# S5 input matrices built in their final layout from factors read back from DRAM, and adaLN pieces summed in PSUM

## The chip, the cores and the metric

One Trainium2 chip, one core. The metric is the device time of one call in microseconds (us). Engines are named as in the profile: PE (TensorE matmul), PEld (its weight load), DVE (VectorE), ACT (ScalarE), POOL (GpSimd), SP (SyncE, which here only issues DMAs).

## What is computed

Two layers of a diffusion backbone over 384 token columns (128 context, 256 latent), width 1024. Layer 0 is half-SwiGLU, S5 mixer, half-SwiGLU; layer 1 has an RG-LRU in the middle. Each sub-layer's shift, scale and gate come from a linear map of the conditioning vector ("adaLN"). What the change touches is the S5 mixer's preparation and that map:

```
abar     = exp(dt * a);  q = (abar - 1) / a           # complex, per direction, group, state
bb       = q[..., None] * b                           # 64 groups x 64 states x 16 inputs
s[t]     = abar * s[t-1] + bb @ u[t]                  # forward and backward
y        = c_re @ s_re - c_im @ s_im + d * u
mod      = silu(cond) @ ada_w + ada_b                 # shift, scale, gate
```

The kernel runs the recurrence in blocks of 8 tokens. For that it needs, for each of the 64 groups, a matrix E (8 x 16 inputs to 64 states of two directions, real and imaginary: powers of abar times bb), a matrix G (states to outputs) and the taps inside a block.

## The kernel before

Matmuls are exact to float32 by splitting each operand into a high and a low part and summing three products (`mm3`, L264 to L266). Weights stream through `raw` buffers (SP queue), ACT makes the high part (L253), DVE the low part (L256). PE's instructions are placed by hand, in program order; the order on DVE, POOL and SP is made by a scheduler from priorities, and each engine executes its queue in that order.

The stage in question is the first feed-forward block, `ffn(0, ...)`. While its matmuls run, a generator `s5_tables` prepares the S5 matrices. Between matmuls `ffn` calls `side()` (made by `beside`): every second k of an up-projection, every third of a down-projection. There are 124 calls before `gen_done()`, which runs the rest of the generator at once, and one more fill comes after it. A call does either one `ada_fill()` (four small matmuls of one adaLN chunk of weights) or one step of the generator, at reduced priority. `beside(125, 42, 9)` means 42 fills spread over 125 calls; the first nine are taken at the even calls 2 to 18.

The generator's steps: three of them (`PRO`) make the elementwise tables (L567 to L684: exp, sine, cosine, powers, `pe`, `pg`, and q in `sn` and `cs`). They are given out before the first matmuls, with no PE work in them. Then come, for 16 chunks of four groups:

- `build_e`: loads `s5bc`, makes bb = q b (six DVE operations of 64 elements per partition, L645 to L650 in `cmul`) and E (six of 512), with states on the partitions;
- `store_e`: eight PE transposes (L731) in two groups of four, two ACT copies (L732), a store to DRAM (`etd`, L734, POOL's queue);
- `taps`: 32 small matmuls (L742) of bb and G, which leave `ks`;
- `build_g`: three DVE and three POOL operations of 640 elements (L716 to L722) and a store (`gd`).

E's buffer (`ech`) exists once, so the next E is written when the transposes have read the last. Nine steps without work stand between the first `build_e` and the first `store_e`; each chunk takes five steps.

`ada_fill` sums the two k-halves of a piece in PSUM, and adds the pieces of a group (four, or two in the first sub-layer) in SBUF: the first by an ACT copy (L151), the others by a DVE addition (L153). Six chunks remain for the S5 stage and are filled there in the middle of its outputs (`ADAS = 4, 2`).

Of the kernel before, what the change touches and what calls it, by code (L numbers as in the profile page):

```python
# [23 lines left out]
Q = 8  # L24
# [10 lines left out]
ADAS = 4, 2  # L35
# [10 lines left out]
def backbone(ctx, tc, a, o):  # L46
# [60 lines left out]
    ada_acc = [None, None, 0]  # L107
# [22 lines left out]
    def ada_fill(n=1, load=True, bank=psaux, flush=True):  # L130


        for _ in range(n):
# [14 lines left out]
            if kh == 1:  # L148
                if j == 0:
# [4 lines left out]
                if j == len(group) - 1:  # L154
                    ada_pend.append((l, s, group, ada_acc[1]))
# [400 lines left out]
    kd = dram.tile([2048, 240], F32, name="kd")  # L556
    td = dram.tile([128, 64, 128], F32, name="td")
# [26 lines left out]
    def s5_tables(gp_):  # L584
# [91 lines left out]
        pe = gp_.tile([128, 2, 8, 64], F32, name="s5pe")  # L676
# [10 lines left out]
        def build_e(ch):  # L687
            g0 = ch * 4
            bc = gp_.tile([128, 4, 64], F32, name="s5bc", tag="bc", bufs=2)
            nc.sync.dma_start(bc, a["s5bc"][ch])  # L690
            ncr = gp_.tile([128, 64], F32, name="s5ncr", tag="ncr")
            V.tensor_scalar(ncr, bc[:, 2, :], -1.0, None, op0=OP.mult)
            bb = gp_.tile([128, 2, 80], F32, name="s5bb", tag="bb", bufs=2)
            G.memset(bb[:, :, 64:80], 0.0)

            qv = lambda t: vw(t, g0, [[1, 4], [0, 16]])
            bv = lambda ri: vw(bc, ri * 64, [[16, 4], [1, 16]])
            ov = lambda ri: vw(bb, ri * 80, [[16, 4], [1, 16]])
            cmul(ov(0), ov(1), qv(sn), qv(cs), bv(0), bv(1), [[16, 4], [1, 16]])

            E = gp_.tile([128, 4, 2, 128], F32, name="s5E", tag="ech")
            pv = lambda ri: vw(pe, ri * 512 + g0, [[1, 4], [64, 8], [0, 16]])
            bv = lambda ri: vw(bb, ri * 80, [[16, 4], [0, 8], [1, 16]])
            ov = lambda ri: vw(E, ri * 128, [[256, 4], [16, 8], [1, 16]])
            cmul(ov(0), ov(1), pv(0), pv(1), bv(0), bv(1), [[128, 4], [16, 8], [1, 16]])
            return bc, ncr, bb, E

        def build_g(ch, bc, ncr):
# [4 lines left out]
            cv = lambda t, j: vw(t, j * 64, [[16, 4], [0, 10], [1, 16]])  # L713
            ov = lambda ri: vw(Gt, ri * 160, [[320, 4], [16, 10], [1, 16]])
            p = [vw(tp, j * 640, [[160, 4], [16, 10], [1, 16]]) for j in range(2)]
            V.tensor_tensor(p[0], cv(bc, 2), pv(0), op=OP.mult)  # L716
            V.tensor_tensor(p[1], cv(bc, 3), pv(1), op=OP.mult)
            V.tensor_tensor(ov(0), p[0], p[1], op=OP.subtract)
            p = vw(tq, 0, [[160, 4], [16, 10], [1, 16]])
            G.tensor_tensor(ov(1), cv(ncr, 0), pv(1), op=OP.mult)  # L720
            G.tensor_tensor(p, cv(bc, 3), pv(0), op=OP.mult)
            G.tensor_tensor(ov(1), ov(1), p, op=OP.subtract)  # L722
            nc.gpsimd.dma_start(gd[ch].rearrange("p (b c) -> p b c", c=128), vw(Gt, 16, [[160, 8], [1, 128]]))
            return Gt

        def store_e(ch, E):
            eo = gp_.tile([128, 1024], F32, name="s5eo", tag="eo")
            for j in range(2):
                pt = psum()
                for b in range(4):  # L730
                    PE.transpose(pt[:, b * 128:b * 128 + 128], E[:, j * 2 + b // 2, b % 2, :], ident)  # L731
                S.activation(eo[:, j * 512:j * 512 + 512], pt, AF.Copy)  # L732
                yield
            nc.gpsimd.dma_start(etd[ch], eo)  # L734

        def taps(ch, bb, Gt):

            kx = (psum(), psum())
            for ri in range(2):
                for d in range(2):  # L740
                    for q in range(4):
                        PE.matmul(kx[d][32 * q:32 * q + 32, 0:128], bb[64 * d:64 * d + 64, ri, q * 16:q * 16 + 32],  # L742
# [8 lines left out]

        cur = build_e(0)
        Gt = build_g(0, *cur[:2])
# [41 lines left out]
    def s5(i, prev):  # L795
        l, s3 = divmod(i, 3)
        with ExitStack() as st:
# [41 lines left out]
            with ExitStack() as st2:  # L839
# [89 lines left out]
                with tc.manual_schedule(engines={ET.Pool}):  # L929
# [5 lines left out]
                    with tc.manual_schedule(engines={ET.DVE, ET.Activation, ET.SP}):  # L935
# [28 lines left out]
                        ada_load(6, nc.sync)  # L964
# [13 lines left out]
                        for part, m in ((f, 0), (f, 1), (f, 2), (s_, 0), (s_, 1), (y, 0), (s_, 2), (f, 3), (f, 4), (y, 1),  # L978
# [3 lines left out]
                            if part is y:  # L982
# [10 lines left out]
                                if m in (2, 3):  # L993
                                    ada_fill(ADAS[m - 2], False, psum, False)
# [350 lines left out]
def _layout(inp):  # L1345
# [34 lines left out]
    gb = lambda v: np.concatenate([v.transpose(1, 0, 2).reshape(64, 16, 4, 16)] * 2, 0)  # L1380
    ct = lambda v: gb(v.transpose(0, 2, 1))
    A["s5bc"] = np.stack([gb(f("s5_b_re")[0]), gb(f("s5_b_im")[0]), ct(f("s5_c_re")[0]), ct(f("s5_c_im")[0])],
# [43 lines left out]
```

## Time and profile before

| | |
|---|---|
| median of 3 runs | 1631.84 us (1628.37 to 1637.66) |
| profiled execution | 1631.38 us, span 1629.6 us |
| PE busy | 1546.1 us (95%) |
| DVE busy | 1278.5 us (78%) |
| ACT busy | 709.4 us (44%) |
| POOL busy | 336.5 us (21%) |
| mean granted PE clock | 0.974 |

A matmul's own duration (0.34 us) overlaps the next; what one costs is the distance from one start to the next. A DVE operation's duration overlaps the next one by some 0.08 us. The granted clock is 1.00 at 2.4 GHz and 0.5 at 1.2 GHz; a figure between is a mean over a stretch.

### The profile page before, as it was taken

To read this page: it belongs to the slowest core of one execution; us is meant where nothing else is said; L and a number is where in the kernel's file an instruction comes from. 1 tells how busy PE (TensorE), PEld (TensorE's weight loads), DVE (VectorE), ACT (ScalarE), POOL (GpSimd) and SP (SyncE) were. 2 spreads that over 40 slices of the span, in tenths; PEclk is the share of its full clock that TensorE was granted. 3 is DMA by queue.
4 is the path that set the end of the run, shared out by engine and by line. 5 is a ranking of instruction groups with operands and counts; after the bars stand their busy time and mean duration, and the time that the engine had idled before them with its cause. 6 is when DMAs were issued, how large, how long until landed. Compare 5 with 4: busy or idle time off the path is not lost.

```text
span 1629.6 us, 25853 instructions
## 1 busy us (share of the span) xinstructions
PE 1546.1 (95%) x9554; PEld 1474.6 (90%) x9554; DVE 1278.5 (78%) x2750; ACT 709.4 (44%) x1157; POOL 336.5 (21%) x524
## 2 busy tenths in 40 slices
PE   7989999999988999999999999999989599999996
PEld 5877887889988999999999999999978599999995
DVE  4999999977796569979777998977797889644445
ACT  4423332335655366333345632334569366323332
POOL 0155445423380013000002300000165322000001
PEclk9989999999999999999999999999999799999997
DMA  9766776877878533667556356755513243544321
GB/s 352 260 215 224 232 244 237 259 244 275 129 272 257 201 133 118 230 202 243 173 171 208 117 188 214 243 193 160 193 64 118 76 157 123 160 153 139 100 77 39
DMA packets 108543, 301.19 MB, mean 185 GB/s; under 512 B 28384, under 2 KB 40160, under 8 KB 108160
## 3 DMA queue, kind: packets, MB, share of 16 engines
q1 hardware_dynamic: 85792, 249.62, 46.3%
q0 software_dynamic: 13152, 46.70, 8.7%
q10 hardware_dynamic: 9472, 3.21, 1.4%
q8 instruction: 75, 1.23, 0.3%
q14 instruction: 52, 0.43, 0.1%
HBM read 275.89 MB, written 27.80 MB: 186 GB/s over the span
## 4 chain that ended last, share of the span: by engine, by line
PE 70%; DVE 20%; DMA 3%; issue 3%; ACT 3%; POOL 1%; SPq 0%; ACTq 0%; DVEq 0%; POOLq 0%
PE mm L264 22%; PE mm L266 22%; PE mm L265 22%; DVE lo L256 2%; DVE hl L317 1%; PE aux L144 1%; DMA adaw<-in_ada_w 1%; DVE s5sb L881 1%; DVE w L878 1%; DVE w L460 1%; ACT w L322 1%; DVE lxc L1090 1%; PE mm L917 1%; DVE s5sb L880 1%; DVE w L879 1%
## 5 line engine op out<-in xcount | busy, mean ns | idle before, releaser
L264 PE MATMUL mm<-hh,hi 128*128 128x384 f32 (+1 forms) x1568 | 542.1, 346 | 14.5 <-DVE hh L1143 7.3
L265 PE MATMUL mm<-hl,hi 128*128 128x384 f32 (+1 forms) x1568 | 535.7, 342 | 10.2 <-DVE hl L317 10.1
L266 PE MATMUL mm<-hh,lo 128*128 128x384 f32 (+1 forms) x1568 | 535.4, 341 | 5.0 <-DVE lo L256 5.0
L253 ACT ACTIVATE hi<-raw 128x1024 fp32r<-128x1024 f32 (+1 forms) x332 | 323.2, 976 | 495.7 <-PE mm L265 467.1
L256 DVE TENSOR_TENSOR lo<-raw,hi 128x1024 fp32r<-128x1024 f32 (+1 forms) x344 | 393.6, 1148 | 164.4 <-ACT hi L253 154.1
L264 PEld LDWEIGHTS mm<-hh,hi 128*128 128x128 f32 x1568 | 298.7, 191 | 32.9 <-issue 15.7
L265 PEld LDWEIGHTS mm<-hl,hi 128*128 128x128 f32 x1568 | 299.0, 191 | 13.3 <-DVE hl L317 12.7
L266 PEld LDWEIGHTS mm<-hh,lo 128*128 128x128 f32 x1568 | 298.6, 190 | 7.0 <-DVE lo L256 7.0
L264 PE MATMUL mm<-zh,hi 128*128 128x384 f32 x704 | 240.5, 342 | 2.0 <-ACT zh L479 2.0
L265 PE MATMUL mm<-zl,hi 128*128 128x384 f32 x704 | 237.5, 337 | 1.8 <-DVE zl L480 1.6
L266 PE MATMUL mm<-zh,lo 128*128 128x384 f32 x704 | 237.0, 337 | 0.0
L264 PEld LDWEIGHTS mm<-zh,hi 128*128 128x128 f32 x704 | 132.9, 189 | 9.6 <-issue 6.3
L179 DVE SCALAR_TENSOR_TENSOR dump<-raw,cb 128x512 bf16<-128x512 f32 x160 | 109.9, 687 | 39.7 <-DMA raw<-in_ada_t 39.2
L265 PEld LDWEIGHTS mm<-zl,hi 128*128 128x128 f32 x704 | 133.1, 189 | 2.6 <-DVE zl L480 2.6
L266 PEld LDWEIGHTS mm<-zh,lo 128*128 128x128 f32 x704 | 133.2, 189 | 0.0
L479 ACT ACTIVATE zh<-w 128x384 fp32r<-128x384 f32 x88 | 46.1, 525 | 160.5 <-DVE w L487 154.1
L179 DVE SCALAR_TENSOR_TENSOR raw<-raw,cb 128x512 f32<-128x512 f32 x160 | 110.1, 688 | 2.6
L395 POOL TENSOR_TENSOR t<-mv 128x3 f32<-128x3 f32 x5 | 4.0, 799 | 446.0 <-ACT mv L394 446.0
L264 PE MATMUL mm<-ph,hi 128*128 128x388 f32 x224 | 77.4, 346 | 0.0
L265 PE MATMUL mm<-pl,hi 128*128 128x388 f32 x224 | 76.6, 342 | 0.0
L266 PE MATMUL mm<-ph,lo 128*128 128x388 f32 x224 | 76.3, 341 | 0.0
L545 DVE SCALAR_TENSOR_TENSOR r<-mm,gate,r 128x128 f32<-128x128 f32 (+1 forms) x144 | 53.2, 410 | 20.5 <-PE mm L266 20.5
(356 smaller groups left out, 1983.1 us busy)
## 6 DMA issues: line engine op xcount, KB each, us to landing
raw<-in_up SPq DMA_DIRECT2D x176, 512.0 KB, 4.4
raw<-in_ada_t SPq DMA_DIRECT2D x80, 512.0 KB, 4.2
raw<-in_down SPq DMA_DIRECT2D x56, 512.0 KB, 3.9
adaw<-in_ada_w POOLq DMA_DIRECT2D x42, 512.0 KB, 5.3
adaw<-in_ada_w SPq DMA_DIRECT2D x22, 512.0 KB, 7.9
raw<-in_down SPq DMA_DIRECT2D x48, 192.0 KB, 2.4
gd<-s5G POOLq DMA_DIRECT2D x16, 512.0 KB, 4.8
etd<-s5eo POOLq DMA_DIRECT2D x16, 512.0 KB, 5.5
```

Of the source, the lines that this page charges most:

```text
L144: PE.matmul(acc[32 * q:32 * q + 32, :256], cond[:, kh * 4 + q, 6 - 2 * j:38 - 2 * j], w[:, q, :], start=kh == 0, stop=kh == 1, tile_positi ...
L179: V.scalar_tensor_tensor(out, wq, 1.0, cb[:, g, q * 512:q * 512 + 512], op0=OP.mult, op1=OP.mult, accum_out=part[:, t, g, q:q + 1])
L253: S.activation(hi[:, :n], raw[:, :n], AF.Copy)
L256: V.tensor_tensor(lo[:, :n], raw[:, :n], hi[:, :n], op=OP.subtract)
L264: PE.matmul(ps, hi[:, c:c + 128], xh, start=start, stop=False)
L265: PE.matmul(ps, hi[:, c:c + 128], xl, start=False, stop=False)
L266: PE.matmul(ps, lo[:, c:c + 128], xh, start=False, stop=stop)
L317: V.tensor_tensor(hl[:, k, :n], src, hh[:, k, :n], op=OP.subtract)
L322: S.activation(h[:, c0:c1], r[:, k, c0:c1], AF.Identity, bias=bs[:, k, g:g + 1], scale=gs[:, k, g:g + 1])
L460: V.scalar_tensor_tensor(t[:, c0:c1], self.ms[:, c0:c1], gw[:, g:g + 1], t[:, c0:c1], op0=OP.mult, op1=OP.add)
L479: S.activation(zh, z, AF.Copy)
L545: V.scalar_tensor_tensor(r[:, m, c0:c1], ps[:, c0:c1], gate[:, m, g:g + 1], r[:, m, c0:c1], op0=OP.mult, op1=OP.add)
```

## The change

- E is made with rows (token in block, input) on the partitions, as it is stored. Its two factors are spread over the partitions by DMA: `pt`, the powers times q, and `bt`, the input b. For `pt` the product `pq` = pe q is made once for all groups, transposed once (eight PE transposes, two ACT copies) and stored to a scratch tensor `ptd`; each chunk then reads its 4 KB row of each of the eight tokens into 16 partitions. E is stored straight from its buffer. The transposes and ACT copies of each chunk are gone.
- bb = q b is made for eight groups at a time (six operations of 128 elements, every second chunk). The negated c moves from DVE to POOL.
- A chunk takes four steps instead of five; two new steps (`pq`; its transposes) stand ahead of the chunks, and six empty steps instead of nine.
- `ada_fill` keeps one PSUM bank over all pieces of a group and empties it once. 40 fills go beside `ffn(0)`, eight into the S5 stage (`ADAS = 4, 4`), with one more chunk loaded ahead and one during the outputs.

```
-ADAS = 4, 2
+ADAS = 4, 4
...
-            if kh == 0:
-                if flush:
-                    ada_flush(bank)
-                ada_acc[0] = bank()
+            if kh == 0 and flush:
+                ada_flush(bank)
             acc = ada_acc[0]
+            begin = acc is None
+            if begin:
+                acc = ada_acc[0] = bank()
+            done = kh == 1 and j == len(group) - 1
+            end = done or close and x == n - 1
...
-                          start=kh == 0, stop=kh == 1, tile_position=(0, 32 * q))
+                          start=begin, stop=end, tile_position=(0, 32 * q))
...
+        pq = gp_.tile([128, 2, 8, 64], F32, name="s5pq", tag="pt")
...
+        cmul(pv(pq, 0), pv(pq, 1), pv(pe, 0), pv(pe, 1), qv(sn), qv(cs), [[64, 8], [1, 64]])
+        yield
+        rows = gp_.tile([128, 2, 4, 128], F32, name="s5rows", tag="ech")
+        for ri in range(2):
+            ps = psum()
+            for b in range(4):
+                PE.transpose(ps[:, b * 128:b * 128 + 128], pq[:, ri, 2 * b:2 * b + 2, :].rearrange("p s g -> p (s g)"), ident)
+            S.activation(rows[:, ri].rearrange("p b c -> p (b c)"), ps, AF.Copy)
+            nc.gpsimd.dma_start(ptd.rearrange("(b s) g r p -> r (s g) b p", s=2)[ri], rows[:, ri])
+        yield
+
+        def load_e(ch):
+            pt = gp_.tile([128, 1024], F32, name="s5pt", tag="pt")
+            nc.sync.dma_start(pt, bass.AP(ptd.tensor, ptd.offset + ch * 1024, [[16384, 8], [0, 16], [1, 1024]]))
+            bt = gp_.tile([128, 512], F32, name="s5bt", tag="bt")
+            nc.sync.dma_start(bt, bass.AP(a["s5bt"].tensor, a["s5bt"].offset + ch * 8192, [[0, 8], [512, 16], [1, 512]]))
+            return pt, bt
...
+            cmul(pv(E, 0), pv(E, 1), pv(pt, 0), pv(pt, 1), bv(0), bv(1), [[128, 4], [64, 2], [1, 64]])
+            nc.gpsimd.dma_start(etd[ch], E.rearrange("p g r c -> p (g r c)"))
...
+            G.tensor_scalar(ncr, two["s5c"][:, 0, ch % 2 * 64:ch % 2 * 64 + 64], -1.0, None, op0=OP.mult)
...
-        for _ in range(9):
+        fac = load_e(0)
+        scaled(0)
+        Gt = build_g(0)
+        for _ in range(6):
             yield
         for ch in range(16):
-            yield from store_e(ch, cur[3])
-            nxt = build_e(ch + 1) if ch < 15 else None
+            build_e(ch, *fac)
+            if ch < 15:
+                fac = load_e(ch + 1)
             yield
-            taps(ch, cur[2], Gt)
             yield
-            if nxt:
-                Gt = build_g(ch + 1, *nxt[:2])
-            cur = nxt
+            taps(ch, two["bb"], Gt)
+            if ch % 2 and ch < 15:
+                scaled(ch // 2 + 1)
+            yield
+            if ch < 15:
+                Gt = build_g(ch + 1)
             yield
...
-                        ada_load(6, nc.sync)
+                        ada_load(7, nc.sync)
...
-                                    ada_fill(ADAS[m - 2], False, psum, False)
+                                    ada_fill(ADAS[m - 2], False, psum, False, True)
+                                    if m == 2:
+                                        ada_load(4, nc.sync)
...
-        norm = ffn(0, (8, 7, 7), None, beside(125, 42, 9), gen_done, first)
+        norm = ffn(0, (8, 7, 7), None, beside(125, 40, 9), gen_done, first)
```

`load2` loads `s5b` and `s5c` for eight groups (128 KB each); `scaled` makes bb from `s5b`.

## Rows read from the trace of the kernel before

**Rows 1.** Busy time by stretch: us, engine busy (count), granted clock, DMA share, GB/s.

```profile
core 0: us, PE busy (x) PEld busy (x) DVE busy (x) ACT busy (x) POOL busy (x), PEclk, DMA share, GB/s
82.00:354.00 272.00, 260.88 (x2022) 227.32 (x2022) 261.46 (x423) 86.77 (x143) 125.36 (x143) 0.97 0.72 235
```

**Rows 2.** Instruction groups of 82 to 354 us, PE's waits: busy, mean ns | idle before.

```profile
L264 PE MATMUL mm<-zh,hi 128*128 128x384 f32 x120 | 45.0, 375 | 2.0 <-ACT zh L479 2.0
L265 PE MATMUL mm<-zl,hi 128*128 128x384 f32 x120 | 42.1, 351 | 1.6 <-DVE zl L480 1.5
L731 PE MATMUL mm<-ident,s5E 128*128 128x128 f32 x120 | 20.3, 289 | 5.5 <-DVE s5E L650 4.7 <-DVE s5E L647 0.8
L193 PE MATMUL aux<-c_sel,adae 128*128 128x8 f32 x20 | 2.8, 250 | 2.0 <-DVE adae L153 2.0
```

**Rows 3.** PE in order of time around a fill and a group of transposes.

```profile
201.47 0.34 PE L265 MATMUL mm<-hl,hi 128*128 128x384 f32 x1
201.64 0.34 PE L266 MATMUL mm<-hh,lo 128*128 128x384 f32 x1
...
202.76 0.34 PE L265 MATMUL mm<-hl,hi 128*128 128x384 f32 x1
...
204.50 0.34 PE L266 MATMUL mm<-hh,lo 128*128 128x384 f32 x1
...
205.30 0.34 PE L265 MATMUL mm<-hl,hi 128*128 128x384 f32 x1
```

**Rows 4.** In order of time: the second side call (a fill), and DVE's table operations.

```profile
56.87 0.64 PE L144 MATMUL aux<-adaw,cond 128*32 128x256 f32 x8
...
59.22 0.22 DVE L608 SCALAR_TENSOR_TENSOR s5t<-s5t,s5t 128x64 f32<-128x64 f32 x1
...
77.86 1.47 DVE L680 COPY s5pe<-s5pw 64x512 f32<-64x512 f32 x1
```

**Rows 5.** DVE's instruction groups, each form apart, up to 354 us.

```profile
L649 DVE TENSOR_TENSOR s5tp<-s5pe,s5bb 128x512 f32<-128x512 f32 x16 | 10.9, 683 | 0.0
L645 DVE TENSOR_TENSOR s5tp<-s5pw 128x128 f32<-128x128 f32 x1 | 0.3, 283 | 0.0
L645 DVE TENSOR_TENSOR s5tp<-s5pw 128x64 f32<-128x64 f32 x1 | 0.2, 217 | 0.0
L692 DVE TENSOR_SCALAR s5ncr<-s5bc 128x64 f32<-128x64 f32 x15 | 5.3, 356 | 0.4 <-DMA s5bc<-in_s5bc 0.4
L153 DVE TENSOR_TENSOR adae<-adae,aux 128x256 f32<-128x256 f32 x14 | 5.8, 411 | 1.1 <-PE aux L144 1.1
L256 DVE TENSOR_TENSOR lo<-raw,hi 128x1024 fp32r<-128x1024 f32 x39 | 50.4, 1296 | 0.4 <-ACT hi L253 0.4
L545 DVE SCALAR_TENSOR_TENSOR r<-mm,gate,r 128x128 f32<-128x128 f32 x16 | 5.5, 343 | 0.0
```

**Rows 6.** DVE and POOL side by side, and POOL's group of 640-element operations.

```profile
213.20 1.85 POOL L720 TENSOR_TENSOR s5G<-s5ncr,s5pg 128x640 f32<-128x640 f32 x1
...
213.89 1.25 DVE L645 TENSOR_TENSOR s5tp<-s5t,s5bc 128x64 f32<-128x64 f32 x1
...
215.21 0.21 DVE L646 TENSOR_TENSOR s5tp<-s5t,s5bc 128x64 f32<-128x64 f32 x1
...
L722 POOL TENSOR_TENSOR s5G<-s5G,s5tq 128x640 f32<-128x640 f32 x16 | 28.5, 1780 | 0.7
```

**Rows 7.** PE near the stage's end: the last taps but one, the last fill.

```profile
353.75 0.67 PE L742 MATMUL mm<-s5G,s5bb 64*32 64x128 f32 x32
...
358.12 0.64 PE L144 MATMUL aux<-adaw,cond 128*32 128x256 f32 x8
```

**Rows 8.** PE in the S5 stage: its second place of fills, two chunks.

```profile
508.83 1.07 PE L144 MATMUL mm<-adaw,cond 128*32 128x256 f32 x16
```

**Rows 9.** DMA issues: count, KB each, median us to landing.

```profile
raw<-etd SPq DMA_DIRECT2D x12, 512.0 KB, 6.6
...
s5bc<-in_s5bc SPq DMA_DIRECT2D x16, 128.0 KB, 3.4
```

More of the change, by code (lines that the diff above doesn't have):

```diff
@@ L128, in ada_load, with ada_fill @@
             ada_loaded.append((c, w, extra))
-    def ada_fill(n=1, load=True, bank=psaux, flush=True):
-        for _ in range(n):
+    def ada_fill(n=1, load=True, bank=psaux, flush=True, close=False):
+        for x in range(n):
             if not ada_loaded:
@@ L153, in ada_fill @@
                     V.tensor_tensor(ada_acc[1], ada_acc[1], acc[:, :256], op=OP.add)
-                if j == len(group) - 1:
-                    ada_pend.append((l, s, group, ada_acc[1]))
+                ada_acc[0] = None
+            if done:
+                ada_pend.append((l, s, group, ada_acc[1]))
+                ada_acc[1] = None
     def vec_pool():
@@ L708, in build_g, with load2, scaled @@
-        def build_g(ch, bc, ncr):
+        two = {}
+        def load2(n, b):
+            two[n] = gp_.tile([128, 2, 128], F32, name=n, tag=n)
+            nc.sync.dma_start(two[n], a[n][b])
+        def scaled(b):
+            bt = two["s5b"]
+            bb = gp_.tile([128, 2, 144], F32, name="s5bb", tag="bb", bufs=2)
+            G.memset(bb[:, :, 128:144], 0.0)
+            qv = lambda t: vw(t, b * 8, [[1, 8], [0, 16]])
+            bv = lambda ri: vw(bt, ri * 128, [[16, 8], [1, 16]])
+            ov = lambda ri: vw(bb, ri * 144, [[16, 8], [1, 16]])
+            cmul(ov(0), ov(1), qv(sn), qv(cs), bv(0), bv(1), [[16, 8], [1, 16]])
+            two["bb"] = bb
+            if b < 7:
+                load2("s5b", b + 1)
@@ L710, in build_g @@
+        def build_g(ch):
             g0 = ch * 4
@@ L712, in build_g @@
             pv = lambda ri: vw(pg, ri * 640 + g0, [[1, 4], [64, 10], [0, 16]])
-            cv = lambda t, j: vw(t, j * 64, [[16, 4], [0, 10], [1, 16]])
+            cv = lambda j: vw(two["s5c"], j * 128 + ch % 2 * 64, [[16, 4], [0, 10], [1, 16]])
             ov = lambda ri: vw(Gt, ri * 160, [[320, 4], [16, 10], [1, 16]])
             p = [vw(tp, j * 640, [[160, 4], [16, 10], [1, 16]]) for j in range(2)]
-            V.tensor_tensor(p[0], cv(bc, 2), pv(0), op=OP.mult)
-            V.tensor_tensor(p[1], cv(bc, 3), pv(1), op=OP.mult)
+            V.tensor_tensor(p[0], cv(0), pv(0), op=OP.mult)
+            V.tensor_tensor(p[1], cv(1), pv(1), op=OP.mult)
             V.tensor_tensor(ov(0), p[0], p[1], op=OP.subtract)
             p = vw(tq, 0, [[160, 4], [16, 10], [1, 16]])
-            G.tensor_tensor(ov(1), cv(ncr, 0), pv(1), op=OP.mult)
-            G.tensor_tensor(p, cv(bc, 3), pv(0), op=OP.mult)
+            ncr = z
+            G.tensor_scalar(ncr, two["s5c"][:, 0, ch % 2 * 64:ch % 2 * 64 + 64], -1.0, None, op0=OP.mult)
+            G.tensor_tensor(ov(1), vw(ncr, 0, [[16, 4], [0, 10], [1, 16]]), pv(1), op=OP.mult)
+            G.tensor_tensor(p, cv(1), pv(0), op=OP.mult)
             G.tensor_tensor(ov(1), ov(1), p, op=OP.subtract)
+            if ch % 2 and ch < 15:
+                load2("s5c", ch // 2 + 1)
             nc.gpsimd.dma_start(gd[ch].rearrange("p (b c) -> p b c", c=128), vw(Gt, 16, [[160, 8], [1, 128]]))
             return Gt
[L726 to L734, printed above, removed]
         def taps(ch, bb, Gt):
@@ L741, in taps @@
                     for q in range(4):
-                        PE.matmul(kx[d][32 * q:32 * q + 32, 0:128], bb[64 * d:64 * d + 64, ri, q * 16:q * 16 + 32],
+                        c0 = ch % 2 * 64 + q * 16
+                        PE.matmul(kx[d][32 * q:32 * q + 32, 0:128], bb[64 * d:64 * d + 64, ri, c0:c0 + 32],
                                   Gt[64 * d:64 * d + 64, q, ri, 32 * d:32 * d + 128],
@@ L1379, in _layout @@
     A["s5a"] = np.concatenate([gp(f("s5_a_re")[0]), gp(f("s5_a_im")[0]), gp(ldt)], 1)
[L1380 removed]
+    gb = lambda v: np.concatenate([v.transpose(1, 0, 2).reshape(64, 8, 128)] * 2, 0)
     ct = lambda v: gb(v.transpose(0, 2, 1))
[L1382 to L1383 removed]
+    bt = lambda v: v.transpose(2, 0, 1).reshape(16, 16, 4, 64)
+    A["s5bt"] = np.stack([bt(f("s5_b_re")[0]), bt(f("s5_b_im")[0])], 3).transpose(1, 0, 2, 3, 4).reshape(16, 16, 512)
+    A["s5b"] = np.stack([gb(f("s5_b_re")[0]), gb(f("s5_b_im")[0])], 0).transpose(2, 1, 0, 3)
+    A["s5c"] = np.stack([ct(f("s5_c_re")[0]), ct(f("s5_c_im")[0])], 0).transpose(2, 1, 0, 3)
     dsk = np.zeros((4, 32, 16), np.float32)
```

37 lines of the change are left out of this document (13 added, 24 removed).

## The prediction

> **What bounds the kernel now.** The views were read in this order: the span in slices, busy time by stretch, the groups of the stretch that the change touches, then single places in order of time. The change lies almost wholly in one stretch, from about 55 us (the first side calls) to 358 us (the last fill); behind it only two fills and a few loads move. In the middle of that stretch, 272 us long, PE is busy for 260.9 us and DVE for 261.5 us [rows 1]. Both are full at once, so a saving on one of them alone need not be a gain. Everywhere else PE leads, and nothing there changes.
>
> PE's waits in the stretch are small and nearly all are for DVE: 5.5 us at the transposes for E, 2.0 us at the flush for the piece sums, 2.0 and 1.6 us for the down-projection's operands [rows 2]. The granted clock is 0.97 there [rows 1], so some 3% of 272 us, 8.2 us, went to half-speed time after such waits. Together 19.3 us.
>
> DVE's busy time holds something that is not work. A 64-element operation takes 0.217 us alone [rows 5], but 1.25 us when it meets a POOL operation that has just started; the next one takes 0.21 us [rows 6]. POOL runs three such operations per chunk, 1.78 us each in the group shown [rows 6], and the change leaves all three in place. So fewer DVE instructions do not shorten these blocked times; they fall on whatever DVE runs then.
>
> **The change, part by part. PE.** In a plain stretch matmuls start every 0.175 us (201.47 to 201.64 is 0.17). From the matmul ahead of a group of four transposes to the second one behind it, 204.50 to 205.30, are 0.80 us, of which two plain distances are 0.35: a group costs 0.45 us. A fill costs in the same way 1.12 - 0.35 = 0.77 us [rows 3]. Removed are 32 groups, 14.4 us; added two, 0.9 us; two fills leave for the S5 stage, 1.5 us. PE's work falls by 15.0 us, and the waits for E (5.5 us) lose their place.
>
> **An early wait on PE.** The transposes of `pq` are the generator's fifth step, which is side call 3. Call 2 is the fill at 56.87 us; with it and 12 matmuls, call 3 stands at about 59.5 us. At 59.22 us DVE is still at the cosine's polynomial; it finishes `pe` at 79.3 us [rows 4]. `pq` is six operations of 512 elements, 0.683 us each [rows 5]: 4.1 us, to 83.4 us. When PE stands still, DVE gets no new feed-forward work once the buffers ahead are full, so the earliest end is some 4 us sooner (the four to five operations of the feed-forward block between 59 and 80 us) and the latest some 3 us later (all of them stay, and POOL blocks twice): 79 to 86. I take 82, which is near the row itself: PE waits 22.5 us. Queued behind on PE is all of the feed-forward block. Nothing of before shows this wait, as the tables had no PE instruction behind them until call 19.
>
> **DVE.** From the tables' end to the last G (about 354 us, just ahead of the taps at 353.75 and 357.5 [rows 7]) DVE was busy 261.5 us of 272 [rows 1]. For the same point after the change:
>
> - bb: 96 operations at 0.217 become 48 at 0.283 [rows 5]: -7.2 us.
> - The negated c leaves DVE: 15 at about 0.2 us undisturbed: -3 us (-5.3 with the blocked time in the row [rows 5]). On POOL it comes back as a short operation that may block DVE: 0 to 5.7 us (16 of the row's 0.356), I take +2, as it has a tenth of the elements of the others.
> - The piece sums: -5.8 us [rows 5]; one ACT copy per group remains, and ACT is busy for a third of the time [rows 1].
> - E keeps its six operations of 512 elements, in another order of addresses: 0, since the forms with stride and with broadcast both go down to 0.68 us. But E of chunk 15 isn't needed for the last taps: -4.1 us.
> - The last taps come earlier in the feed-forward block. A chunk takes four generator steps, not five; with 40 fills in 125 calls, taps 15 are generator step 71 and side call 104, while before the last G fell to call 123. DVE must by then have done the block's work of calls 3 to 104 (101 calls), where before it was calls 12 to 123 (111). That work is six groups, from 50.4 to 5.5 us [rows 5], 103 us in all, 0.93 us a call: -9 us.
>
> Sum: 261.5 - 27 = 234.5 us busy. The 10.5 us that DVE was idle may go or stay; I take half: 240 (234 to 245). From 82 us this ends at 322 us. PE needs less: it stood at call 3 at 82 us, and its work to call 104 is about 217 us (54 calls of 12 matmuls, 47 of 7 or 8, 32 fills, 16 taps at 0.8): 299 us. So the taps wait for DVE, and PE stands at call 104 at 322 us. What is queued behind the taps on PE is the feed-forward block; DVE itself starts ahead in it only as far as its buffers.
>
> **The rest of the block.** From call 104 to the fill of call 125 PE has 21 calls of 12 matmuls (44 us), 7 fills (5.4 us) and taps (0.8 us): 50 us. The end is 372 us against 358.1 [rows 7]: +14 us. The S5 stage takes two more chunks at its second place, where two took 1.07 us between outputs [rows 8]: +1.1 us (0 if the two DVE sums that vanish there were what PE waited for, 1.9 at the half clock). Together +15: 1631.4 + 15 = 1646 us. The profiled execution (1631.38) lies 0.5 us under the median, so nothing is corrected.
>
> **Loads.** Each chunk reads 768 KB for `pt` and `bt` in place of 128 KB for `s5bc`. `pt` is loaded when E has read the last one; until the next E DVE has G, taps and feed-forward work, 240 / 16 - 4.1 = 10.9 us. A 512 KB read of a scratch tensor lands after 6.6 us, a 128 KB load after 3.4 [rows 9]. I take 7 to 10 us, so the load is covered, at no cost; it decides from about 10 us.
> The Trainium skill ("DMA: Bandwidth & Descriptors", on why a DMA increments its semaphore by 16, and the rules for kernel authors) speaks against these two loads: a DMA is split over as many engines as divide its slowest dimension, and an outer broadcast of 8 keeps it on at most 8 of 16. No run here shows such a load; by that rule the two would take longer than the rows say, and the third rival below would be the case.
>
> **The rivals.** *PE sets the pace.* If DVE's blocked times shrink with its load, or the scheduler puts E behind the block's own operations, PE runs freely after the early wait. From 59.5 to 358.1 it took 298.6 us; less 15.0 us of work and the 19.3 us of waits and slow clock is 264.3; from 82 us this ends at 346.3, 11.8 us early, with the S5 stage +1.1: 1621 us. For it: PE's own work does fall, and E no longer stands on its way. Against: DVE is full in [rows 1], and would have to get through about 10% less than the sum says.
> *The same, without the early wait*, if the scheduler brings the tables forward: 22.5 us less, 1598 us. Against: DVE was as full before 59 us as behind it.
> *The factors come late.* If `pt` and `bt` land 12 us after the last E, each E and all DVE work behind it starts 2 us later: 15 chunks, 30 us: 1676 us. It decides where landing passes about 10 us; against it stand the medians of [rows 9], for it that the block's loads share the engines.
> That the change doesn't do what it says has no place here: the instructions are gone from the code.
>
> **How the numbers follow.** DVE sets the pace: 0.50, 1646 us, its own range 1633 to 1659 (DVE's sum 234 to 245, the early wait 79 to 86, POOL's extra operation). PE sets the pace: 0.27, 1614 to 1629. Without the early wait: 0.07. Late factors: 0.16, 1655 to 1685. A measurement of this kernel tells about 0.5%, 8 us, from no change. Faster by more than that (under 1623.7): 0.19 of the second case and 0.07, 0.26. Slower (over 1640): 0.40 of the first and 0.16, 0.56. Between: 0.18. The range leaves out about one in ten on either side: 1612 (the third case and the low end of the second) to 1668 (the upper half of the last).
>
> **What would show it.** Right: a PE gap of some 20 us near 60 us, ended by `pq`'s transposes; DVE at 95% or more until the last G; PE waits at the taps or at the low parts between 120 and 320 us; no generator work behind call 104, and some 50 us of undisturbed matmuls after it; E's operations without waits for a DMA. Wrong: no gap at 60 us, or a gap and then no further one; E's first operation waiting for `pt`; blocked DVE operations much rarer than before.

## The result: 80 us slower

The changed kernel takes 1711.49 us (median of 4 runs, 1709.07 to 1713.29) against 1631.82 us (4 runs, 1628.37 to 1637.66): ratio 1.0482, 95% interval 1.0461 to 1.0502. The forecast was 1646 us with a range of 1612 to 1668: the direction was right, the size was not.

The first reading is where the 82 us between the two profiled spans (1629.6 and 1711.5 us) arise. A mark that both kernels have is the sums for the next normalisation, twelve matmuls at the end of the feed-forward block and again at the end of the S5 stage. Before:

```profile
393.37 1.50 PE L388 MATMUL aux<-omean,sum 128*128 128x1 f32 x12
...
600.35 1.50 PE L388 MATMUL aux<-omean,sum 128*128 128x1 f32 x12
```

After (PE in order of time):

```profile
471.25 1.50 PE L394 MATMUL aux<-omean,sum 128*128 128x1 f32 x12
...
682.68 1.50 PE L394 MATMUL aux<-omean,sum 128*128 128x1 f32 x12
```

So 77.9 us are lost in the feed-forward block with the tables, 4.4 us in the S5 stage (207.0 became 211.4 us), and nothing behind it (1029.3 and 1028.8 us to the end). In the stretch of [rows 1] both engines that were full are now idle for a fifth of the time, and the granted clock is 0.88 where it was 0.97 (busy time by stretch, columns as there):

```profile
82.00:354.00 272.00, 216.58 (x1592) 183.80 (x1592) 215.63 (x295) 54.44 (x92) 122.97 (x133) 0.88 0.70 223
```

PE's and DVE's waits between 50 and 460 us say for what (line waited for: us in total, times, longest). PE, against [rows 2]:

```profile
PE mm L726 <- DVE s5pq L654: 23.2, 1, 23.2
PE mm L270 <- ACT zh L485: 17.0, 3, 7.1
PE mm L270 <- DVE w L493: 16.6, 4, 10.2
PE aux L148 <- DMA adaw<-in_ada_w: 11.1, 3, 6.9
```

DVE:

```profile
DVE s5tp L652 <- DMA s5bt<-in_s5bt: 48.6, 12, 8.8
DVE lo L262 <- ACT hi L259: 33.9, 14, 5.2
```

The first line of PE is the forecast early wait. The first line of DVE is the one that the forecast's sum gave no price to: L652 is the first operation of E, and in 12 of 16 chunks it waits for bt (in chunk 0 for pt, 1.9 us). One chunk in order of time (SP's issues, DVE's operations):

```profile
257.74 0.60 SPq L734 DMA_DIRECT2D s5pt<-ptd  x1
258.43 0.61 SPq L736 DMA_DIRECT2D s5bt<-in_s5bt  x1
...
257.74 0.69 DVE L657 TENSOR_TENSOR s5E<-s5tp 128x512 f32<-128x512 f32 x1
...
262.19 0.83 DVE L757 TENSOR_TENSOR s5G<-s5tp 128x640 f32<-128x640 f32 x1
270.49 0.69 DVE L652 TENSOR_TENSOR s5tp<-s5pt,s5bt 128x512 f32<-128x512 f32 x1 [7.48 <-DMA s5bt<-in_s5bt]
```

The loads go out when E has read the last factors, and bt lets DVE go on 12.1 us after its issue (258.43 to 270.49). In between DVE does what stands ahead of E, then stands still for 7.5 us with the feed-forward block's operations queued behind E. pt is not what holds it: by the trace's landing records, pt lands 7.0 us after its issue here and bt, issued 0.7 us behind it, after 11.9. Over all 16 loads of each the medians are 7.8 us for pt (6.4 to 10.3) and 10.5 us for bt (8.2 to 13.1). PE's waits for `zh` and `w` are read as the echo. The loop's pace and the end of the block follow from it (line: count, shortest/median/longest ns, first to last start): the last step of E, the taps, the fills.

```profile
L657 DVE TENSOR_TENSOR s5E<-s5tp x16: 678/692/1820, 103.4 to 385.1; 128x512 f32<-128x512 f32 x16
L776 PE MATMUL mm<-s5G,s5bb x512: 266/269/419, 137.3 to 384.1; 64*32 64x128 f32 x171
L148 PE MATMUL aux<-adaw,cond x448: 379/403/637, 5.0 to 436.7; 128*32 128x256 f32 x150
```

A chunk takes (385.1 - 103.4) / 15 = 18.8 us. The last matmul of the taps starts at 384.1 (357.9 before), that of the fills 52.6 us later, at 436.7 ([rows 7]: 358.1). The forecast was 322 and 372.

### The profile page after: what moved, and what is told of

The parts are those of the page before. It is cut to its first block, busy times and chain, and to the rows that moved or that the text cites. A ratio compares the mean times of both kernels' runs of the same rounds, so it can differ in the third digit from the quotient of the medians.

```text
span 1711.5 us, 25534 instructions
## 1 busy us (share of the span) xinstructions
PE 1549.9 (91%) x9434; PEld 1473.7 (86%) x9434; DVE 1277.8 (75%) x2671; ACT 690.4 (40%) x1127; POOL 346.0 (20%) x532
## 4 chain that ended last, share of the span: by engine, by line
PE 60%; DVE 16%; DMA 5%; issue 3%; ACT 2%; POOL 2%; SPq 0%; ACTq 0%; DVEq 0%; POOLq 0%
PE mm L270 19%; PE mm L272 19%; PE mm L271 19%; DMA s5bt<-in_s5bt 3%; DVE lo L262 2%; DVE hl L323 1%; DMA etd<-s5E 1%; DVE s5sb L919 1%; DVE w L466 1%; DVE w L916 1%; DVE lxc L1130 1%; PE mm L955 1%; DVE r L436 1%; DVE r L437 1%; DVE s5sb L918 1%
## 5 line engine op out<-in xcount | busy, mean ns | idle before, releaser
L262 DVE TENSOR_TENSOR lo<-raw,hi 128x1024 fp32r<-128x1024 f32 (+1 forms) x344 | 402.9, 1176 | 188.3 <-ACT hi L259 177.4
```

Source lines behind the costliest of these rows:

```text
L262: V.tensor_tensor(lo[:, :n], raw[:, :n], hi[:, :n], op=OP.subtract)
```

## The experiments

Times are medians beside runs of the kernel before on the same chip (1632.8 to 1634.0 us). "Mark" is the first of the sums above (393.4 before, 471.3 after). e1, e2, e3, e5, e6 and e7 ran once each. Runs of the kernel before lie between 1628 and 1638 us, so among these six a difference of a few us shows nothing. The theory at the start: late loads cost most of the 65 us beyond the forecast, and they are late because of their shape; the rivals: E's place in DVE's order or DVE's own pace, and the early wait.

**e1, no loads after the first chunk.** `if ch < 15: fac = load_e(ch + 1)` is left out, and with it the right factors for 15 chunks.

> The changed kernel, but the factors (pt and bt) are loaded for chunk 0 alone; E of the other fifteen chunks is computed from the same factors, so fifteen loads of each are left out and those chunks' tables hold other numbers. Late loads (my theory now): in the changed kernel a chunk takes 18.8 us, of which some 11 to 12 are the landing of the loads; without them the cycle falls to DVE's own 15 us (240 us over 16 chunks), 16 x 3.8 = 61 us less, 1645 to 1660 us. Rival, the order of the instructions on DVE (E standing ahead of feed-forward work, whatever it waits for) or POOL's blocking sets the cycle: less than 15 us are gained, over 1695 us.

1668.0 us, mark 426.4. The loads cost 43 us, less than the 50 to 65 expected, and both theories named a part. The lines of E, the taps and the fills:

```profile
L657 DVE TENSOR_TENSOR s5E<-s5tp x16: 677/688/1704, 103.5 to 338.0; 128x512 f32<-128x512 f32 x16
L776 PE MATMUL mm<-s5G,s5bb x512: 269/269/420, 130.9 to 339.3; 64*32 64x128 f32 x171
L148 PE MATMUL aux<-adaw,cond x448: 379/379/637, 5.1 to 391.8; 128*32 128x256 f32 x150
```

A chunk now takes 15.6 us, near the 15 expected for DVE's own pace. But 33 us of the 78 remain in the block, where I had forecast 14, and no load is left to blame.

**e2, the transposes of pq later.** Six generator steps later (the expectation calls them side calls; with the fills between they are more calls), first chunk as before:

```diff
-        yield
+        for _ in range(7):
+            yield
         rows = gp_.tile([128, 2, 4, 128], F32, name="s5rows", tag="ech")
...
-        for _ in range(6):
-            yield
+        yield
         for ch in range(16):
```

> The changed kernel with the transposes of pq six side calls later; the chunks start at the same call as before, so everything is computed. If the early wait of 23 us on PE adds to the rest, the time falls by 15 to 23 us, to 1688 to 1696 us. Rival: the chain of loads and E sets when the block ends, and it starts at the same time as before or later, so that the wait only moves from 60 us to the taps: within 8 us of 1711 us, or slower by the up to 10 us by which the first factors come later.

1708.7 us, mark 465.7: the early wait is gone from PE's list, and 31.3 us of waits for G stand at the taps in its place (1.3 in the changed kernel). The time is 2.8 us less, which a single run does not tell from no change. DVE's chain sets the end, and its end moved by 5 us:

```profile
L657 DVE TENSOR_TENSOR s5E<-s5tp x16: 678/691/2132, 114.9 to 380.3; 128x512 f32<-128x512 f32 x16
```

A wait of 25 us on PE that stands ahead of a stretch paced by DVE was not a cost of its own.

**e3, the same loads with a slowest dimension of 16.** ptd is stored twice (c = 0, 1), bt comes repeated from DRAM:

```diff
-  bass.AP(ptd.tensor, ptd.offset + ch * 1024, [[16384, 8], [0, 16], [1, 1024]])
+  bass.AP(ptd.tensor, ptd.offset + ch * 1024, [[16384, 16], [0, 8], [1, 1024]])
-  bass.AP(a["s5bt"].tensor, ..., [[0, 8], [512, 16], [1, 512]])
+  a["s5bt"][ch]
```

> The changed kernel, everything computed, but the slowest dimension of both factor loads counts 16 and more in place of 8: ptd is stored twice by the two halves of a channel group, so that pt is read as 16 x 8 rows, and bt comes repeated from DRAM as 128 plain rows; bytes written to SBUF are the same. If the loads are late because they run on 8 of the 16 DMA engines, landing falls from 11 to 12 us to 6 to 8 us, the chunk cycle from 18.8 to 15 or 16 us, and the time to 1650 to 1680 us. Rival, they are late because of 768 KB per chunk, of what else is in the queues, or because pt can only be read again once E has read it: landing stays above 10 us and the time within 15 us of 1711 us.

1683.7 us, mark 441.0: 28 us back for the same bytes into SBUF. The DMA list (KB each, median us to landing) and E's line:

```profile
s5pt<-ptd SPq DMA_DIRECT2D x16, 512.0 KB, 6.1
s5bt<-in_s5bt SPq DMA_DIRECT2D x16, 256.0 KB, 6.5
...
L657 DVE TENSOR_TENSOR s5E<-s5tp x16: 678/689/1937, 112.1 to 354.8; 128x512 f32<-128x512 f32 x16
```

Landing falls from 7.8 to 6.1 us for pt and from 10.5 to 6.5 for bt, the chunk from 18.8 to 16.2 us. DVE still waits 15.2 us for bt and 4.7 for pt. The Trainium skill ("DMA: Bandwidth & Descriptors", rules for kernel authors) says that an outermost dimension of c < 16, such as a leading broadcast of c copies, keeps a DMA on at most c engines. The trace agrees: in the changed kernel each factor load has eight landing records (behind one that comes 1 us after the issue), here each has sixteen.

**e5 and e6, both edits in pairs.** e5 is e1 with the late transposes, e6 is e3 with them.

> Both former edits at once: factors loaded for chunk 0 alone (fifteen loads of each left out, those chunks' tables hold other numbers) and the transposes of pq six side calls later. With the loads in place the move was worth 3 us. If the early wait costs time of its own once no load sets the pace, the time falls from 1668 us by 18 to 25 us to 1643 to 1650 us. Rival: DVE, 49 of 50 us busy between 150 and 300 us without the loads, sets the end whatever PE does at 60 us; then it stays within 8 us of 1668 us.

> Everything computed: transposes of pq six side calls later, and both factor loads with a slowest dimension of 16 and more. If the 20 us that DVE still waits for factors in the wide kernel (15.2 for bt, 4.7 for pt) keep the chain of loads and E in charge, the move is worth as little as before: 1675 to 1684 us. If the chain is no longer in charge: 1655 to 1666 us.

1666.4 us against e1's 1668.0, and 1680.3 against e3's 1683.7. With no load in the way (e5) the rival held, and e6 lies in its first range: removing the early wait is worth 1.6 and 3.4 us, no more than the spread of single runs. DVE, not PE's start, sets the end.

**e7, loads a chunk ahead.** As e6; E is computed in place over pt (`pv` are its real and imaginary parts), which frees the memory for two buffers of each factor, and the load of the chunk after next is issued behind G:

```diff
-            E = gp_.tile([128, 4, 2, 128], F32, name="s5E", tag="ech")
+            V.tensor_tensor(p[0], pv(0), bv(0), op=OP.mult)
+            V.tensor_tensor(p[1], pv(0), bv(1), op=OP.mult)
+            V.tensor_tensor(pv(0), pv(1), bv(1), op=OP.mult)
+            V.tensor_tensor(pv(0), p[0], pv(0), op=OP.subtract)
+            V.tensor_tensor(pv(1), pv(1), bv(0), op=OP.mult)
+            V.tensor_tensor(pv(1), pv(1), p[1], op=OP.add)
...
-                fac = load_e(ch + 1)
+                fac.append(load_e(ch + 2))
```

> Everything computed: as the former kernel, and E is written over pt, so that pt and bt have two buffers each in the same memory and are loaded a chunk ahead. DVE's waits for factors fall from 20 us to under 4 us. If the waiting of E is all that loads cost, the time is that of the kernel without loads and with late transposes, within 8 us. Rival: the 11.5 MB more of reads crowd the stores and weight loads of the block; then it stays 12 us or more above it.

1665.9 us, the time of e5 without any loads. One wait of 5.1 us for the first pt is left. So nearly the whole price of the loads is that E waits for them; a price of the traffic of the wide loads does not show within a single run's spread.

**e8, five steps per chunk.** A further `yield` in twelve of sixteen chunks.

> As the former kernel, but twelve of the sixteen chunks take five generator steps, as in the kernel before, so that the last tables come near call 120 and not call 104. By my sum DVE's work for the tables and the block fell from 261 to about 250 us when it is spread over all 125 calls, and PE's by 15 us; if the four steps per chunk were what put DVE in charge, the time falls below the kernel before, to 1615 to 1632 us. Rival: DVE's idle and blocked times do not depend on where the steps stand: within 8 us of the kernel with four steps.

1651.4 us (ratio 1.0107, 1.0083 to 1.0130): 14.5 us back, less than hoped. The four steps are the forecast's own term: the taps end too early in the calls, and a tail of plain matmuls follows. e8's last taps start at 368.8 and its last fill at 373.7, where e7's were at 341.1 and 388.3. What is left stands at the front (PE in order of time):

```profile
117.47 0.69 PE L271 MATMUL mm<-zl,hi 128*128 128x384 f32 x1 [7.39 <-DVE zl L486]
...
144.15 1.11 PE L784 MATMUL mm<-s5G,s5bb 64*32 64x128 f32 x32 [11.69 <-DVE s5G L765]
```

DVE stood still for 7.5 us in front of them: E of chunk 0 waits for pt at 116.3, 26 us after pq was ready at 90.2 (transposes, eight stores on POOL's queue, the load).

**e10, E behind the taps of the next chunk.** The transposes also stand two steps earlier, with two steps more between them and the first chunk.

```diff
         for ch in range(16):
-            build_e(ch, *fac.pop(0))
+            if ch:
+                build_e(ch - 1, *fac.pop(0))
             yield
             yield
             taps(ch, two["bb"], Gt)
...
+        build_e(15, *fac.pop(0))
```

> The kernel with loads ahead and five steps, but E of a chunk stands behind the taps of the next chunk in program order, the transposes of pq come one step earlier and their way through DRAM to the first E has about five steps more. In the five-step kernel PE still waits 20.8 us between 109 and 144 us, behind a first E that waits 7.5 us for pt, 26 us after pq was ready. If that first round trip is what is left, these waits fall below 7 us and the time to 1630 to 1638 us. Rival: G and the feed-forward work are late on DVE whatever E does; the waits move and the time stays above 1645 us.

1638.7 us (1.0041, 1.0026 to 1.0056), 12.7 us less than e8 and just above the 1630 to 1638 expected. PE's 20.8 us between 109 and 144 have become one wait of 6.6 us there, and 9.3 us at the transposes.

**e4, e9, e15: what the rest of the change does.** e4 is the changed kernel with E made and transposed as before. e9 is the kernel before with the piece sums in PSUM and their fills moved. e15 is e4 with 42 fills in the block and 4 and 2 in the S5 stage, as before.

> The changed kernel with E made and transposed per chunk as in the kernel before (no factor loads, no pq); q B for eight groups, the negated c on POOL and the piece sums in PSUM stay. If the loss lies in the new E alone: DVE's sum falls by 7.2 us for q B, 3 us for c and 5.8 us for the sums, PE's work hardly changes, the S5 stage is about 1 to 4 us longer for its two more fills; 1618 to 1636 us. Rival: q B in blocks of eight, the single buffers of the b and c tiles (the c tile is loaded again only when G has read it) or POOL's extra operation cost the time: above 1645 us.

> The kernel before with one part of the change alone: pieces summed in PSUM, 40 fills in the block and 4 and 4 in the S5 stage (with its loads). In the changed kernel and in the one with E as before, the S5 stage is 4.3 to 4.4 us longer than before, where I had forecast 1.1 us. If these fills are the cause, this kernel's S5 stage is longer by 4 us too, the block saves 0 to 4 us (DVE 5.8 us, PE 1.5 us), and the time is 1632 to 1637 us. If the stage is longer because of something in the tables: the stage as before and 1627 to 1632 us.

> E made and transposed per chunk as before, with q B for eight groups, the negated c on POOL, the piece sums in PSUM and 42 fills in the block. The same kernel with 40 fills was level with the kernel before with an S5 stage 4.3 us longer. If that is the price of the moved fills: 1627 to 1631 us, 0.1 to 0.3% faster than before. Rival: the fills cost the block as much as they save the S5 stage: 1631 to 1634 us.

1632.6 us (ratio 0.9997, 0.9986 to 1.0008), 1637.1 us (1.0025, 1.0015 to 1.0034), and 1635.7 us (1.0013, 1.0000 to 1.0027). So q B, the negated c and the sums are no loss and no gain together, and all of the 80 us comes with the new E, its loads and its four steps per chunk. The piece sums with their moved fills cost 4 us: e9's S5 stage takes 212.2 us, its mark is at 394.6. e15 missed its 1627 to 1631: its S5 stage is short (207.6), but its block is 3 us longer than e4's. Over the profiles the S5 stage is 207.9 to 212.2 us in eleven kernels with 40 fills (median 211.7) and 206.2 to 210.1 in nine with 42 (median 207.0): some 4 to 5 us, with overlap (e10 has 207.9 with 40, e11 210.1 with 42). The traces show what goes with the two lengths. It is one group of 32 matmuls some 130 us behind the mark, before and after:

```profile
522.30 3.78 PE L917 MATMUL aux<-al,raw 128*128 128x98 f32 x32 [1.29 <-ACT s5Y L921]
...
602.54 5.41 PE L955 MATMUL aux<-al,raw 128*128 128x98 f32 x32 [2.15 <-ACT hh L988]
```

In all twelve kernels whose stage takes 209.9 us or more, PE waits longer for ACT ahead of this group, and the group takes 5.4 us; the granted clock of the 20 us around it, from 120 us behind the mark, is 0.91, so part of them ran at 1.2 GHz. In all eight at or under 208.2 us the group takes 3.8 us, at a clock of 1.00. Nine of the eleven kernels with 40 fills are of the long kind, and three of the nine with 42. Why ACT is later there is not shown.

**e11 and e12: 42 fills, and the loads' shape once more.** e11 is e10 with 42 fills (and ten chunks of five steps); e12 is e11 with the loads and stores of the change, slowest dimension 8.

> As the former kernel with 42 fills in the block and 4 and 2 in the S5 stage, as in the kernel before (pieces still summed in PSUM; ten chunks of five steps in place of twelve). If the two moved fills cost the S5 stage 4.3 us and give the block 1.5 us: 2 to 4 us faster than the former kernel. Rival: the block is bound by DVE and fills cost it more than their 0.77 us: no gain, or up to 3 us slower.

> As the former kernel with the factor loads and stores as in the change (slowest dimension 8, ptd stored once by two DMAs). If a slow landing of 11 to 12 us matters only where E stands behind it, a load one chunk of 15 us or more ahead hides it: within 4 us of the former kernel, or a little faster by six fewer DMA issues on the way to the first E. Rival: loads on 8 engines hold up the block's other transfers for longer: 8 us or more slower.

e11: 1631.4 us (0.9990, 0.9978 to 1.0002), 7.2 us less than e10, more than the 2 to 4 expected, and level with the kernel before. e12: 1641.3 us (1.0059, 1.0041 to 1.0077), 9.9 us slower than e11, as the rival said and not as expected. DVE waits 12.4 us for pt (2.8 in e11), and 8.7 of these stand at one place, the last E, at 345.6 us. Its load went out at 334.4, so it was not early: the last chunks take four steps. PE waits 6.3 us behind it. At the taps of chunk 14 the profile of e12 is 1.6 us behind that of e11 (338.7 against 337.1), at the last taps 10.6 (362.7 against 352.0). The block's other transfers are late too: PE's fills wait 9.0 us for their pieces (2.2 in e11), POOL 31.0 us for c (11.8 in e11). Up to chunk 14 these waits left no more than the 1.6 us. So the expectation that a load a chunk ahead hides a slow landing is not refuted; it failed where the load was not ahead.

**e13, e14, e16: the last waits.** e14 is e11 with the transposes two steps later (eight chunks of five steps). e13 is e14 with two tiles for the taps' results and one for bt. e16 is e13 with one step, not three, between the transposes and the first chunk.

> As the kernel with E behind the taps, wide loads and 42 fills (1631.4 us), with the transposes of pq two generator steps later (chunks two steps later too, eight chunks of five steps) and two tiles for the taps' results (bt goes back to one buffer, loaded right behind E). If the waits left on PE add to the end of the block: 9.3 us of the early wait and some 5 us of ACT's and PE's waits behind the results' store fall away, 1617 to 1625 us, faster than the kernel before. Rival: PE and DVE are both full, and a wait that goes here comes back there: 1628 to 1634 us.

> As the former kernel without the second tile for the taps' results (and with two buffers for bt). If the early wait is what is left: 1619 to 1627 us, within 3 us of the former. If the tile of the results is the cause: 4 to 8 us slower than the former.

> As the kernel with later transposes and two tiles for the results, but only one generator step between the transposes and the first chunk in place of three (ten chunks of five steps). The first E would meet its factors some 4 to 6 us earlier in program order and wait for pt: if DVE's wait there stops PE, 3 to 8 us slower than the former; if E stands far enough behind the taps: within 2 us.

1638.1 us (1.0026, 1.0013 to 1.0039), 1632.9 us (1.0001, 0.9988 to 1.0015) and 1637.2 us (1.0019, 1.0005 to 1.0033). In e14 the early wait is gone, and PE waits 9.9 us for `zl` at 119.7 in its place. It stands behind E of chunk 0, for which DVE waits 10.2 us for pt (2.8 in e11): later transposes leave less time for the way through DRAM. None of the three reached the gain expected of it. e13 is slower than its rival's 1628 to 1634 us, e14 is faster than e13 by 5.2 us where it should have been level or slower, which no run explains, and e16 is level with e13. PE has about 15 us less work than before, by the forecast's count, and no gain from it.

**e17 and e18: G's imaginary part on DVE.** Why is DVE full, with less to do? In e14 these are POOL's three operations of G and the negated c, and two of DVE's groups for q B (busy us, mean ns), 55 to 360 us:

```profile
L771 POOL TENSOR_TENSOR s5G<-s5G,s5tq 128x640 f32<-128x640 f32 x16 | 31.6, 1973 | 0.9
L770 POOL TENSOR_TENSOR s5tq<-s5c,s5pg 128x640 f32<-128x640 f32 x16 | 25.1, 1571 | 0.1
L768 POOL TENSOR_SCALAR s5t<-s5c 128x64 f32<-128x64 f32 x16 | 9.1, 571 | 13.7 <-DMA s5c<-in_s5c 11.2 <-DVE s5tp L748 2.2 <-DVE s5pw L644 0.3
...
L654 DVE TENSOR_TENSOR s5bb<-s5tp 128x128 f32<-128x128 f32 x8 | 6.6, 831 | 0.2
L655 DVE TENSOR_TENSOR s5tp<-s5t,s5b 128x128 f32<-128x128 f32 x8 | 4.8, 598 | 0.2
```

With the third product (25.3 us) POOL works 91 us there, and operations of 128 elements that take 0.28 us alone [rows 5] stand for 0.6 to 0.8 us. e17 is e14 with these operations on DVE; e18 is the kernel before with its three:

```diff
-            G.tensor_tensor(ov(1), cv(ncr, 0), pv(1), op=OP.mult)
-            G.tensor_tensor(p, cv(bc, 3), pv(0), op=OP.mult)
-            G.tensor_tensor(ov(1), ov(1), p, op=OP.subtract)
+            V.tensor_tensor(p[0], cv(ncr, 0), pv(1), op=OP.mult)
+            V.tensor_tensor(p[1], cv(bc, 3), pv(0), op=OP.mult)
+            V.tensor_tensor(ov(1), p[0], p[1], op=OP.subtract)
```

> As e14 (1632.9 us), with the three POOL operations of G per chunk and the negated c computed on DVE, into DVE's own scratch. DVE gets 16 x 3 operations of 640 elements at 0.74 us from start to start and 16 small ones, 38 us more. If POOL's operations are what blocks DVE, at least 55 of the 85 us by which its operations stand longer than undisturbed go; DVE gains some 20 us or more, and PE, with 15 us less work than before, can follow: 1612 to 1626 us. Rival: those 85 us are waits for PE, ACT and the loads; then DVE's 38 us come on top, and the time is 1650 to 1675 us.

> The kernel before with the three POOL operations of G per chunk on DVE, nothing else. DVE gets 35.5 us more. If the 83 us of blocked time are POOL's doing, DVE is freed by 25 to 45 us, and PE loses most of its 9 us of waits and 8 us of slow clock: 1612 to 1625 us. Rival as for e17: 1650 to 1670 us. If e17 is faster than e18, the new E is worth its place once DVE is free (PE has 15 us less work there); if not, it isn't.

1623.3 us (0.9942, 0.9925 to 0.9959) and 1622.7 us (0.9941, 0.9924 to 0.9958): both beat both kernels. DVE got 48 operations of 0.82 us more, 39.5 us, and is less busy for it. Stretch 82 to 354 us of e14, then of e17, then of e18:

```profile
82.00:354.00 272.00, 246.07 (x1927) 214.09 (x1922) 249.03 (x353) 69.13 (x119) 143.77 (x159) 0.96 0.85 283
```

```profile
82.00:354.00 272.00, 258.30 (x2013) 224.68 (x2006) 239.85 (x423) 76.26 (x127) 62.13 (x106) 0.97 0.88 288
```

```profile
82.00:354.00 272.00, 263.70 (x2117) 230.70 (x2110) 247.32 (x472) 91.26 (x152) 53.31 (x99) 0.99 0.73 240
```

DVE's 239.85 us less the 39.5 new ones are 200 us, where it was 249: some 49 us of its busy time in e14 were POOL's doing, less than the 55 expected. q B's operations in e17:

```profile
L654 DVE TENSOR_TENSOR s5bb<-s5tp 128x128 f32<-128x128 f32 x8 | 2.3, 289 | 0.2
L655 DVE TENSOR_TENSOR s5tp<-s5t,s5b 128x128 f32<-128x128 f32 x8 | 2.3, 291 | 0.2
```

The Trainium skill ("SBUF — State Buffer", who interferes with whom) says that a DVE instruction with two SBUF inputs contends with a POOL instruction that reads SBUF, for a read interface that they share and that one holds exclusively. 831 ns falling to 289 agrees. e17 and e18 are equal within their intervals: even with DVE freed, the new E (with the rest of the change) is worth no more than the old one as far as these runs took it. In e17 DVE still waits 15.5 us for c and 4.2 us for the first pt; what E would be worth without these waits is not shown.

The ledger of the block is the mark's way back, each kernel keeping the edits of the one before it except where told: 471.3 us after, 441.0 with wide loads (e3), 422.9 with loads ahead and late transposes (e7), 408.2 with five steps (e8), 397.8 with E behind the taps (e10), 394.9 with 42 fills and still later transposes (e14), 381.6 with G on DVE (e17); 393.4 in the kernel before, 384.4 in e18.

## Why the prediction was wrong, step by step

**The loads: the step that failed.** The text set a landing of 7 to 10 us against 10.9 us of other work on DVE and took "7 to 10 us, so the load is covered, at no cost". The landing was not far off: 7.8 us for pt, inside the range, and 10.5 for bt, just outside it. [rows 9] are loads of another shape and were used as if they held for these; the sentence beside them named the rule that spoke against it. What was wrong by far is the slack. A chunk's 15 us less E's 4.1 are a mean, and they count work that does not stand between one E and the next in DVE's order: the block's operations run between E's own six, too. In e1, with no loads, the time from the end of one E to the start of the next is 8.4 us in the mean and goes from 4.0 to 17.2; in 11 of 15 chunks it is under 10.9. Two neighbours (e1, DVE; the last operation of one E, the first of the next):

```profile
207.84 0.69 DVE L657 TENSOR_TENSOR s5E<-s5tp 128x512 f32<-128x512 f32 x1
212.84 0.68 DVE L652 TENSOR_TENSOR s5tp<-s5pt,s5bt 128x512 f32<-128x512 f32 x1
...
217.46 0.69 DVE L657 TENSOR_TENSOR s5E<-s5tp 128x512 f32<-128x512 f32 x1
218.18 1.30 DVE L652 TENSOR_TENSOR s5tp<-s5t,s5b 128x128 f32<-128x128 f32 x1
...
229.16 0.69 DVE L652 TENSOR_TENSOR s5tp<-s5pt,s5bt 128x512 f32<-128x512 f32 x1
```

The first gap is 4.3 us, the second, with q B in it, 11.0. An estimate from e1's 15 gaps, each short of a landing of 10.5 us by what it is short, gives 46 us of waiting; DVE waited 48.6 us for bt. With e3's 6.5 us it gives 12 us, against 15.2 measured, and the forecast's own 7 to 10 us would give 16 to 41. So the cost was there even inside the forecast's range, and the shape made it larger.

The rival of the late factors got 0.16, and it is what happened. Its price was too low: 2 us for each of 15 chunks, 30 us, again from a mean, where the runs give 42 to 43 (1711.5 to 1668.0 in e1, 1708.7 to 1666.4 with the late transposes). The first operation of E holds up in order all of the block's operations behind it, so most of DVE's 50.5 us of waiting for factors became time of the kernel.

**DVE's sum: mis-sized, by 17 us at the last taps.** Without loads (e1) the last taps are at 339.3, not at 322. From 82 to 339 us DVE is busy for 241.3 us, not 234.5, and idle for 15.7, not 5.5. The busy part is the blocked time that "falls on whatever DVE runs then": q B saves 10 us (34.8 against 44.9 us for its groups), but `lo`, 1.30 us in [rows 5], takes 1.58 us in e1, over 32 of them 9 us (1.22 us in e17, where POOL's operations are gone). The step named that and then did not subtract it. It also called DVE full from 82 us on; e8 and e10 show that at the front it waits for the first factors and for E's place in its order.

**The tail of the block: right.** Forecast 50 us from call 104 to the last fill; 52.5 in e1 (339.3 to 391.8), 52.6 after. e8 shows that the four steps per chunk make it, and that it can be given back.

**The early wait: right, and rightly not added.** Forecast 22.5 us with transposes from 82 us (79 to 86); measured 23.2 and 2.1 us, transposes from 83.1 (PE in order of time, after):

```profile
59.53 0.34 PE L272 MATMUL mm<-hh,lo 128*128 128x384 f32 x1
83.08 1.09 PE L726 MATMUL mm<-ident,s5pq 128*128 128x128 f32 x4 [23.21 <-DVE s5pq L654]
86.26 1.09 PE L726 MATMUL mm<-ident,s5pq 128*128 128x128 f32 x4 [2.10 <-DVE s5pq L657]
```

The sum let DVE start at 82 us either way and did not pay for PE's wait. e2, e5 and e6 agree: moving the transposes changes single runs by 1.6 to 3.4 us, not by 23. The two rivals in which PE sets the pace (1621 and 1598 us) did not come about.

**The S5 stage: mis-sized.** Forecast +1.1 us for two fills, measured +4.4 after and some 4 to 5 us over the kernels with 40 fills. The fills' own work is near the forecast, for the second place holds 32 matmuls in 1.93 us against 16 in 1.07 [rows 8]; of the rest, 1.6 us are the group that ran partly at 1.2 GHz (5.41 against 3.78 us), which comes 2.4 us later behind the mark than before.

**PE's 15 us: never on the path.** No run contradicts that the work is gone, but e11 and e14 lack it too and are level with the kernel before, and e17 and e18 are equal. In these kernels the saving on PE shows only as waits elsewhere, for what DVE makes.

**The sum again.** In the block 77.9 us: 14 forecast, 45 for the loads (mark 471.3 to 426.4 in e1), 17 more for DVE up to the last taps, 2.5 more in the tail; these make 78.5. With the S5 stage's 4.4 this is the difference of the spans.

## What to carry to other kernels

Before a load is called covered, look at its shape as well as its size, and count what stands between its issue and its use in the engine's own order, chunk by chunk: a mean hides the short gaps, and on a full engine a late operand costs the whole queue. A saving counts only on the engine that sets the end; here PE's saving brought nothing, and the waits moved in e13, e14 and e16 came back elsewhere until DVE itself was freed. When one engine's operations last several times their undisturbed length, take the other engine's work away first, even by giving it to the blocked one.

## What the runs showed of the hardware that was not expected

A load of 512 KB and one of 256 KB, issued 0.7 us behind it, landed 7.8 and 10.5 us after issue (medians) with a slowest dimension of 8, and 6.1 and 6.5 us with 16 or more, for the same bytes written. Beside the slow shape other loads landed later: `raw<-in_down` 9.0 us after issue in e12, 5.3 in e11 (medians, 60 to 390 us). Moving 91 us of POOL's work to DVE made DVE less busy: 249.0 to 239.9 us of 272, with 39.5 us more to do.
